# Order of the output accumulators in memory, and the activations of the first three groups, in a one-core decoder block

## The chip, the core and the metric

The kernel runs on one core of a Trainium2 chip. Its engines are TensorE (PE, matrix products into the accumulator memory PSUM; PEld is its weight load), VectorE (DVE), ScalarE (ACT), GpSimd (POOL) and SyncE (SP, which only issues transfers). Each has its own instruction queue and takes it strictly in order; they wait for each other by semaphores. The metric is the device time of one execution in microseconds, lower being better.

## The reference

One decoder block on 512 tokens of width 2048, all in float32. A pooling mixer and a stick-breaking attention are merged and added to `x`; what matters here is the squared-ReLU MLP at the end, with `w_ff1` of 2048 x 8192 and `w_ff2` of 8192 x 2048:

```
h2 = rms_norm(x, norm2_w[l]) * (1.0 + scale2[:, None]) + shift2[:, None]
f = jnp.square(jax.nn.relu(h2 @ w_ff1[l])) @ w_ff2[l]
x = x + gate2[:, None] * f
```

## The kernel before

**Precision and products.** A float32 operand is split into a high and a low part (`split_into`, lines 138 and 139: ScalarE writes `hi`, VectorE writes `lo = src - hi`), and a product is the sum of three, hi·hi, lo·hi and hi·lo. Both MLP products are done on 2 x 2 blocks with seven block products in place of eight (numbers `i` = 1, 7, 3, 6, 2, 5, 4; `PERIOD` sets that order), on sums of weight blocks (made by VectorE at line 1376 and by GpSimd's accumulating transfers at line 1354) and sums of activation blocks (`S`).

**Units.** The work is a list of units; a unit is one block product. For each unit `n` the main loop at the end of the kernel writes, in this order: what follows the unit before (`units[n-1].after()`), the split of the weights for unit `n+2` (`prep`; the ring of split weights has three places), one step of every open generator in the list `later` (`steps()`), and the matmuls of unit `n`. So an instruction that waits on ScalarE or VectorE holds up the weight splits behind it, and with three places in the ring TensorE runs dry about two units later.

**First product.** It makes 32 groups of 256 hidden columns. Groups 0 to 2 (`FIRST` = 3) are made together by all eight products into banks named `C`, while the sums `S` are still being formed (`first_units`). `after()` at its end puts the ReLU of these three groups into tiles `hr` and appends one `finish` generator each to `later`. `finish` has three steps: squares on ScalarE (line 1150), three VectorE sums (lines 1152 to 1155), then the store of `hr` to the DRAM buffer `hd` (line 1157; from ScalarE's queue, and for the last group from GpSimd's). From group 3 on the seven products follow, each of eight pairs of matmuls (lines 1176 and 1178). `M` is a product's bank. Product 6 adds to the bank of product 1, and product 5 to that of 6, so each needs ScalarE's copy of the partial result first (line 1183: `p`, `z`, `u` after products 1, 7 and 6).

**Second product.** It runs over eight chunks `c` of 1024 hidden rows and two column pairs `n`; a product is two units of 12 matmuls each (lines 303 to 305). Its operands `S` are read back from `hd`. The results are summed in eight accumulators `acc2[m, b]`, each 4 KiB per partition, where `m` is the column pair and `b` one of `"11", "21", "12", "22"`. The first chunk is written by a ScalarE copy (line 1317), and later products are added by VectorE (line 1319). `open_sums` makes the accumulators in memory that the first product's pool `evac` gives back: two `hr` buffers of 8 KiB, five small copies (`p`, `z`, `u`), and the tile `c` of 8 KiB. A new tile waits only for those old tiles whose bytes it covers. In the pool, accumulators lie in the order in which they are made; first written in the run are (0, 11), (0, 22), (0, 21), (1, 11), (1, 22), (0, 12), (1, 21), (1, 12). The last group's `hr` is in the first of the two `hr` buffers, at the pool's lowest bytes.

Of the kernel before, what the change touches and what calls it, by code (L numbers as in the profile page):

```python
# [10 lines left out]
F32 = mybir.dt.float32  # L11
# [5 lines left out]
P = 128  # L17
T = 512
# [78 lines left out]
def block_kernel(ctx: ExitStack, tc: tile.TileContext, x, c, w_ada, b_ada, norm1_w, w_in, q_norm_w,  # L97
                 k_norm_w, w_pool, pool_scale, w_a_up, w_b_up, w_o, norm2_w, w_ff1, w_ff2, out):
    nc = tc.nc
# [15 lines left out]
    def name_of(name):  # L115
        count[0] += 1
        return f"{name}_{count[0]}"
# [864 lines left out]
    NP, GROUPS, CH, CP = 8, 32, 8, 4  # L982
    FIRST = 3
# [15 lines left out]
    hd = dram.tile([GROUPS, P, 7, 256], F32, name="hd")  # L999
# [28 lines left out]
    later = []  # L1028

    def steps():  # L1030
        for s in list(later):
            if next(s, s) is s:
                later.remove(s)
# [34 lines left out]
    def first_units():  # L1068
        banks = {}

        def before(m):
            def go():
                s = m // 2
                if m % 2 == 0:
                    if s < 3:
                        scale_bias(s + 1)
                    if s:
                        split_x(s - 1, ((7, 0), (6, 1), (5, 3)))
                else:
                    if s < 3:  # L1080
                        split_x(s + 1, AS_IS)
                    sums_x(s)
                    if s == 2:
                        split_x(0, ((3, 2),))
                        split_x(1, ((3, 2),))
            return go

        def part(wh, wl, at, g, m):

            for row in range(2):  # L1090
                if m == 0:
                    banks[g, row] = bank.tile([P, 2, 256], F32, tag="bank", name=name_of("C"))
                for k in range(2):
                    i = ((1, 2), (3, 4))[row][k]
                    hi, lo = (S[i, m // CP][:, a, m % CP, :] for a in range(2))
                    for q in range(2):
                        cols = slice((at + 2 * k + q) * P, (at + 2 * k + q + 1) * P)
                        products(banks[g, row][:, q, :], wh[:, cols], wl[:, cols], hi, lo, m == k == q == 0,
                                 m == NP - 1 and k == 1, skip_group_check=True)

        def mm(m):
            def go(wh, wl):
                for g in range(2):
                    part(wh, wl, 4 * g, g, m)
            return go

        def mm2(m):
            def go(wh, wl):
                for e in range(2):
                    part(wh, wl, 4 * e, 2, m + e)  # L1110
            return go

        def after():
            def relu(g, hr):
                nc.scalar.activation(hr[:, 1:3, :], banks[g, 0], AF.Relu)
                nc.scalar.activation(hr[:, 0:4:3, :], banks[g, 1], AF.Relu)
                later.append(finish(g, hr))
            relu(0, h_tile(0))
            split_x(3, ((7, 0), (6, 1), (5, 3)))
            split_x(2, ((3, 2),))  # L1120
            split_x(3, ((3, 2),))
            xts.close()
            pools["evac"] = pool(ffr, "evac", 1, "right")
            relu(1, h_tile(1))
            relu(2, h_tile(3))

        def src(gm):
            def load(raw, _):
                for i, (g, m) in enumerate(gm):
                    nc.sync.dma_start(raw[:, i * T:(i + 1) * T].rearrange("p (q n) -> p q n", n=P),  # L1130
                                      w_ff1[g, :, :, m, :].rearrange("q p n -> p q n"))
            return load

        made_of = []
        for m in range(NP):
            made_of.append(Unit(0, (0, m), src(((0, m), (1, m))), mm(m), None, before(m)))
            if m % 2:
                made_of.append(Unit(0, (0, m, 2), src(((2, m - 1), (2, m))), mm2(m - 1),
                                    after if m == NP - 1 else None))
        return made_of  # L1140
# [3 lines left out]
    def h_tile(g):  # L1144

        return (pools["evac"] if g % 2 else hrp).tile([P, 8, 256], F32, tag="hr", bufs=1 + g % 2, name=name_of("hr"))

    def finish(g, hr):

        nc.scalar.activation(hr[:, 0:4, :], hr[:, 0:4, :], AF.Square)  # L1150
        yield
        nc.vector.tensor_tensor(hr[:, 4:6, :], hr[:, 1:4:2, :], hr[:, 0:1, :].broadcast_to([P, 2, 256]),
                                op=ALU.subtract)
        nc.vector.scalar_tensor_tensor(hr[:, 6, :], hr[:, 5, :], -1.0, hr[:, 1, :], op0=ALU.mult, op1=ALU.subtract)
        nc.vector.scalar_tensor_tensor(hr[:, 7, :], hr[:, 2, :], -1.0, hr[:, 6, :], op0=ALU.mult, op1=ALU.subtract)
        yield
        (nc.gpsimd if g == GROUPS - 1 else nc.scalar).dma_start(hd[g], hr[:, 1:8, :])


    def ff1_units(first):  # L1160
# [70 lines left out]
    keep, acc2 = {}, {}  # L1231
# [34 lines left out]
    def ff2_units(gn, i):  # L1266
        c, n = divmod(gn, 2)
        st = ff2_state.setdefault(gn, {})
        name = {1: "11", 2: "11", 6: "21", 4: "21", 5: "22", 7: "22", 3: "12"}[i]
        new = i in (1, 7, 2)  # L1270
        last = gn == 2 * CH - 1 and i == 3

        def open_sums():
            while later:
                steps()
            ffr.close()
            accp = pool(ffr, "acc2", 1, "right")
            for m in range(2):
                for b in ("11", "21", "12", "22"):
                    acc2[m, b] = accp.tile([P, 2, T], F32, name=f"acc_{m}{b}")  # L1280

        def mm_of(half):
            def mm(wh, wl):
                if "bank2" not in pools:
                    ffb.close()
                    pools["bank2"] = pool(ffb, "bank2", 4, space=PSUM)
                if half == 0:
                    if gn == 0 and len(made) < 7:
                        next_first()
                    if new:  # L1290
                        st[CHAIN[i]] = pools["bank2"].tile([P, 2, T], F32, tag="bank", name=name_of("M"))
                    if last:
                        a = acc2[n, name]
                        nc.vector.tensor_tensor(a, a, gated(2 * n + 1), op=ALU.mult)
                        nc.vector.tensor_tensor(a, keep[0, 2 * n + 1], a, op=ALU.subtract)  # L1295
                if half and n == 1 and c + 1 < CH:
                    make_s(i, c + 1)
                for t in range(2):
                    for k in range(2):
                        hi, lo = (S[i, c][:, a, 2 * half + k, t * P:(t + 1) * P] for a in range(2))  # L1300
                        cols = slice(k * T, (k + 1) * T)
                        products(st[CHAIN[i]][:, t, :], hi, lo, wh[:, cols], wl[:, cols], new and half == k == 0,
                                 half == k == 1, skip_group_check=not new)
            return mm

        def after():
            if not acc2:
                open_sums()
            ps, a = st[CHAIN[i]], acc2[n, name]
            if last:  # L1310
                for t in range(2):
                    nc.vector.tensor_tensor(ps[:, t, :], ps[:, t, :], keep["g", 2 * n + 1], op=ALU.mult)  # L1312
                    nc.vector.tensor_tensor(a[:, t, :], a[:, t, :], ps[:, t, :], op=ALU.subtract)  # L1313
                    nc.sync.dma_start(out[t * P:(t + 1) * P, T * (2 * n + 1):T * (2 * n + 2)], a[:, t, :])
                return
            if c == 0 and i in (1, 6, 7, 3):
                nc.scalar.activation(a, ps, AF.Copy)
            else:
                nc.vector.tensor_tensor(a, ps, a, op=ALU.add)  # L1319
            if c == CH - 1 and i in (2, 4, 5, 3):  # L1320
                put(0 if i in (2, 3) else 1, 2 * n + (i in (5, 3)), a)
            if gn == 0:
                load_s(i, 1)
            if n == 1 and c + 2 < CH:
                load_s(i, c + 2)
            elif n == 1 and c + 2 == CH and i in (1, 7, 6, 2, 5):
                hold((1, 7, 6, 2, 5).index(i), i)

        def src_of(half):
            return lambda raw, q: w_ff2[c, n, q, :, 2 * half:2 * half + 2, :].rearrange("p m n -> p (m n)")  # L1330
        return [Unit(i, (2, gn, half), src_of(half), mm_of(half), after if half else None) for half in range(2)]
# [122 lines left out]
```

## Time and profile before

| what | value |
|---|---|
| median of 3 runs | 2504.03 us (2501.37 to 2513.46) |
| the profiled execution, whole | 2503.11 us |
| its span, first to last instruction | 2501.4 us |
| mean granted TensorE clock | 0.994 |
| PE, DVE, ACT, POOL busy | 98%, 73%, 45%, 6% of the span |

The profile is of one execution. TensorE is busy in almost all of the span, so what counts is the few stretches in which it stands still or is granted less than its full clock. In the views below a row's bracket tells how long that engine stood idle just before the row, and what ended the idle time.

### The profile page before, as it was taken

Reading aid. Unit: us, or ns where it says so; the run is one execution under the profiler, and the core shown is the slowest. Engines: PE = TensorE matmul, PEld = TensorE weight load, DVE = VectorE, ACT = ScalarE, POOL = GpSimd, SP = SyncE. Lnnn points to the kernel's source line nnn. Section 1 sums busy time; section 2 is a strip of 40 time slices with the busy share of each in tenths; the row PEclk is TensorE's granted clock in tenths of the full one; section 3 lists DMA queues with packets and bytes.
Section 4 is the critical chain, followed back from the end, with each engine's and each line's share of the span. In section 5 each row is a group of like instructions: output and inputs, shape, how many; then the busy total and the mean of one; then the engine's idle time right before and its main releaser. Section 6 shows DMA issues by size and latency. Waiting matters only on the chain. (4 is left out here: it accounts for less than half of the span.)

```text
span 2501.4 us, 32636 instructions
## 1 busy us (share of the span) xinstructions
PE 2458.4 (98%) x12387; PEld 2055.6 (82%) x12387; DVE 1837.5 (73%) x2303; ACT 1134.1 (45%) x1552; POOL 155.7 (6%) x234
## 2 busy tenths in 40 slices
PE   8999999999999999999999999999998999999998
PEld 5777888888888888888888888888886888888886
DVE  5888555555667666665577777777786889888889
ACT  5222556653223222433455555555555444444452
POOL 0000011100000000000000100001010100100100
PEclk9999999999999999999999999999998999999999
DMA  9873222223667667576447777777787777877775
GB/s 314 267 244 98 88 68 69 75 79 108 227 221 233 227 226 239 192 235 228 127 130 200 208 210 216 211 210 203 212 256 230 212 227 211 219 201 207 214 224 150
DMA packets 246037, 482.48 MB, mean 193 GB/s; under 512 B 16684, under 2 KB 111972, under 8 KB 245880
## 3 DMA queue, kind: packets, MB, share of 16 engines
q1 hardware_dynamic: 222232, 382.80, 46.6%
q0 software_dynamic: 19184, 69.15, 14.8%
q10 hardware_dynamic: 4464, 28.44, 2.8%
q8 instruction: 97, 1.59, 0.3%
q14 instruction: 60, 0.49, 0.1%
HBM read 442.59 MB, written 37.75 MB: 192 GB/s over the span
## 5 line engine op out<-in xcount | busy, mean ns | idle before, releaser
L139 DVE TENSOR_TENSOR flo<-raw,fhi 128x1024 fp32r<-128x1024 f32 x439 | 534.4, 1221 | 213.9 <-ACT fhi L138 213.7
L138 ACT ACTIVATE fhi<-raw 128x1024 fp32r<-128x1024 f32 x439 | 464.4, 1058 | 395.5 <-PE M L305 295.7
L1176 PE MATMUL M<-S,fhi 128*128 128x512 f32 x1624 | 566.3, 395 | 3.7 <-ACT u L1183 3.1
L138 ACT ACTIVATE whi<-raw 128x512 fp32r<-128x512 f32 x388 | 236.9, 627 | 487.3 <-PE ps L304 148.5
L1178 PE MATMUL M<-S,flo 128*128 128x256 f32 x1624 | 451.2, 278 | 0.0
L139 DVE TENSOR_TENSOR wlo<-raw,whi 128x512 fp32r<-128x512 f32 x388 | 263.4, 690 | 214.1 <-ACT whi L138 213.1
L1176 PEld LDWEIGHTS M<-S,fhi 128*128 128x128 f32 x1624 | 305.9, 188 | 75.5 <-ACT u L1183 3.5
L303 PE MATMUL M<-fhi,S 128*128 128x512 f32 x896 | 349.8, 390 | 11.0 <-ACT fhi L138 11.0
L303 PE MATMUL ps<-hh,whi 128*128 128x512 f32 x896 | 354.9, 396 | 2.2 <-ACT whi L138 2.2
L304 PE MATMUL M<-flo,S 128*128 128x512 f32 x896 | 350.3, 391 | 1.6 <-DVE flo L139 1.6
L305 PE MATMUL ps<-hh,wlo 128*128 128x512 f32 x896 | 350.0, 391 | 0.0
L304 PE MATMUL ps<-hl,whi 128*128 128x512 f32 x896 | 349.6, 390 | 0.0
L305 PE MATMUL M<-fhi,S 128*128 128x512 f32 x896 | 349.5, 390 | 0.0
L1178 PEld LDWEIGHTS M<-S,flo 128*128 128x128 f32 x1624 | 306.4, 189 | 0.0
L408 DVE SCALAR_TENSOR_TENSOR ada<-raw,sc,ada 128x512 f32<-128x512 f32 (+1 forms) x296 | 207.2, 700 | 41.7 <-DMA raw<-in_w_ada_dram 34.8
L303 PEld LDWEIGHTS M<-fhi,S 128*128 128x128 f32 x896 | 168.9, 188 | 46.5 <-ACT fhi L138 11.4
L303 PEld LDWEIGHTS ps<-hh,whi 128*128 128x128 f32 x896 | 168.4, 188 | 42.7 <-issue 6.5
L304 PEld LDWEIGHTS M<-flo,S 128*128 128x128 f32 x896 | 168.7, 188 | 39.0 <-DVE flo L139 4.4
L305 PEld LDWEIGHTS ps<-hh,wlo 128*128 128x128 f32 x896 | 168.4, 188 | 36.5 <-DVE wlo L139 0.3
L305 PEld LDWEIGHTS M<-fhi,S 128*128 128x128 f32 x896 | 168.8, 188 | 35.1
L304 PEld LDWEIGHTS ps<-hl,whi 128*128 128x128 f32 x896 | 168.6, 188 | 33.4
L1354 POOL DMA_DIRECT2D raw<-in_w_ff_dram x122 | 107.4, 953 | 1136.8 <-DVE raw L1376 439.1
(260 smaller groups left out, 3214.5 us busy)
## 6 DMA issues: line engine op xcount, KB each, us to landing
raw<-in_w_ff_dram SPq DMA_DIRECT2D x244, 512.0 KB, 5.2
raw<-in_w_ada_dram SPq DMA_DIRECT2D x128, 512.0 KB, 4.4
raw<-in_w_ff_dram POOLq DMA_DIRECT2D x122, 512.0 KB, 7.7
raw<-in_w_in_dram SPq DMA_DIRECT2D x94, 512.0 KB, 4.1
raw<-in_w_ada_dram SPq DMA_DIRECT2D x128, 256.0 KB, 5.9
S<-hd SPq DMA_DIRECT2D x56, 512.0 KB, 6.9
hd<-hr ACTq DMA_DIRECT2D x31, 896.0 KB, 3.6
raw<-in_w_in_dram SPq DMA_DIRECT2D x64, 256.0 KB, 3.1
```

The costliest lines, as they stand in the source:

```text
L138: nc.scalar.activation(hi, src, AF.Copy)
L139: nc.vector.tensor_tensor(lo, src, f(hi), op=ALU.subtract)
L303: nc.tensor.matmul(ps, lhsT=lh, rhs=rh, start=start, stop=False, **kw)
L304: nc.tensor.matmul(ps, lhsT=lh, rhs=rl, start=False, stop=False, **kw)
L305: nc.tensor.matmul(ps, lhsT=ll, rhs=rh, start=False, stop=stop, **kw)
L408: nc.vector.scalar_tensor_tensor(s, raw, sc[:, k:k + 1], before, op0=ALU.mult, op1=ALU.add)
L1176: nc.tensor.matmul(ps, lhsT=wh[:, cols], rhs=both, start=new and m == 0, stop=False, skip_group_check=not new)
L1178: nc.tensor.matmul(ps[:, 256:T], lhsT=wl[:, cols], rhs=both[:, 0, :], start=False, stop=m == NP - 1, skip_group_check=not new)
L1354: nc.gpsimd.dma_start(raw[u.key, what], u.src(None, q), accum_op=ALU.add)
```

## The change

Three edits. `open_sums` makes the eight accumulators in another order, so that each lies at another place of the same 32 KiB. `finish` takes a number of empty steps to pass before the squares, 0, 2 and 4 for groups 0, 1 and 2. And the stores of groups 0 to 2 are issued by GpSimd.

```
-            relu(0, h_tile(0))
+            relu(0, h_tile(0), 0)
...
-            relu(1, h_tile(1))
-            relu(2, h_tile(3))
+            relu(1, h_tile(1), 2)
+            relu(2, h_tile(3), 4)
...
-    def finish(g, hr):
-
+    def finish(g, hr, wait=0):
+
+        for _ in range(wait):
+            yield
...
-        (nc.gpsimd if g == GROUPS - 1 else nc.scalar).dma_start(hd[g], hr[:, 1:8, :])
+        (nc.gpsimd if g < FIRST or g == GROUPS - 1 else nc.scalar).dma_start(hd[g], hr[:, 1:8, :])
...
-            for m in range(2):
-                for b in ("11", "21", "12", "22"):
-                    acc2[m, b] = accp.tile([P, 2, T], F32, name=f"acc_{m}{b}")
+            for m, b in ((1, "12"), (1, "21"), (1, "22"), (0, "12"), (1, "11"), (0, "21"), (0, "22"), (0, "11")):
+                acc2[m, b] = accp.tile([P, 2, T], F32, name=f"acc_{m}{b}")
```

The program has the same instructions; TensorE's and SyncE's orders stay as they were. ScalarE where groups 0 to 2 end and group 3 begins, before (`hr_11267`, `hr_11284` and `hr_11287` are groups 0, 1 and 2; `fhi` are weight splits):

```order
L138 ACTIVATE fhi_11290<-raw_10788 128x1024
L1150 ACTIVATE hr_11267<-hr_11267 128x1024
L1150 ACTIVATE hr_11284<-hr_11284 128x1024
L1150 ACTIVATE hr_11287<-hr_11287 128x1024
L1183 ACTIVATE p_2173_11314<-M_11297 128x512
L138 ACTIVATE fhi_11316<-raw_10854 128x1024
L1183 ACTIVATE z_2178_11350<-M_11333 128x512
L138 ACTIVATE fhi_11352<-raw_10720 128x1024
L1157 DMA hd<-hr_11267 128x1792
L1157 DMA hd<-hr_11284 128x1792
L1157 DMA hd<-hr_11287 128x1792
L1183 ACTIVATE u_2182_11377<-M_11297 128x512
```

and now, where lines from 1150 on carry a number two higher:

```order
L138 ACTIVATE fhi_11290<-raw_10788 128x1024
L1152 ACTIVATE hr_11267<-hr_11267 128x1024
L1185 ACTIVATE p_2173_11312<-M_11295 128x512
L138 ACTIVATE fhi_11314<-raw_10854 128x1024
L1185 ACTIVATE z_2178_11342<-M_11325 128x512
L138 ACTIVATE fhi_11344<-raw_10720 128x1024
L1152 ACTIVATE hr_11284<-hr_11284 128x1024
L1185 ACTIVATE u_2182_11368<-M_11295 128x512
L138 ACTIVATE fhi_11370<-raw_10788 128x1024
L138 ACTIVATE fhi_11398<-raw_10908 128x1024
L1152 ACTIVATE hr_11287<-hr_11287 128x1024
```

Two of the three squares moved behind the copies `p` and `z` and the splits between them, and the three stores left this queue. GpSimd at the same place, before (sums of weight blocks by transfer):

```order
L1354 DMA raw_10788<-in_w_ff_dram 128x1024
L1354 DMA raw_10720<-in_w_ff_dram 128x1024
L1354 DMA raw_10977<-in_w_ff_dram 128x1024
L1354 DMA raw_10908<-in_w_ff_dram 128x1024
L1354 DMA raw_11356<-in_w_ff_dram 128x1024
```

and now:

```order
L1355 DMA raw_10977<-in_w_ff_dram 128x1024
L1159 DMA hd<-hr_11267 128x1792
L1159 DMA hd<-hr_11284 128x1792
L1355 DMA raw_10908<-in_w_ff_dram 128x1024
L1159 DMA hd<-hr_11287 128x1792
L1355 DMA raw_11348<-in_w_ff_dram 128x1024
```

The stores stand in front of the weight sums of the next groups. On VectorE each group's three sums moved with its square: the two splits that stood behind all nine sums now stand behind the first three. ScalarE where the second product begins, before, with the semaphores that each instruction waits for (`hr_2932` is the last group; `acc_011` is the accumulator (0, 11)):

```order
L1190 ACTIVATE hr_2932_16394<-hr_2932_16394 128x512 [waits DVE_49]
L1191 ACTIVATE hr_2932_16394<-hr_2932_16394 128x512
L1150 ACTIVATE hr_2932_16394<-hr_2932_16394 128x1024 [waits Activation_49]
L1317 ACTIVATE acc_011_16444<-M_2933_16402 128x1024 [waits DVE_49,DMASW4_49,PE_49,Activation_49]
L138 ACTIVATE fhi_2937_16455<-raw_2896_16177 128x1024
L1220 ACTIVATE S2_2919_16306<-S2_2919_16306 128x1024 [waits DMAHW2_49]
L138 ACTIVATE fhi_2940_16474<-raw_2907_16230 128x1024 [waits PE_49]
L1317 ACTIVATE acc_022_16447<-M_2939_16461 128x1024 [waits PE_49]
```

and now:

```order
L1192 ACTIVATE hr_2932_16394<-hr_2932_16394 128x512 [waits DVE_49]
L1193 ACTIVATE hr_2932_16394<-hr_2932_16394 128x512
L1152 ACTIVATE hr_2932_16394<-hr_2932_16394 128x1024 [waits Activation_49]
L1318 ACTIVATE acc_011_16451<-M_2933_16402 128x1024 [waits PE_49]
L138 ACTIVATE fhi_2937_16455<-raw_2896_16177 128x1024
L1222 ACTIVATE S2_2919_16306<-S2_2919_16306 128x1024 [waits DMAHW7_49]
L138 ACTIVATE fhi_2940_16474<-raw_2907_16230 128x1024 [waits DVE_49,PE_49]
L1318 ACTIVATE acc_022_16450<-M_2939_16461 128x1024 [waits PE_49]
```

The order is the same; the copy into (0, 11) no longer names the semaphore of GpSimd's transfer (DMASW), on which the last group's store reports. In the new order (1, 12) and (1, 21) lie where that group's `hr` was.

## Rows read from the trace of the kernel before

**Rows 1.** The page: span, TensorE's busy time (us, share, instructions), one group of part 5.

```profile
span 2501.4 us, 32636 instructions
...
PE 2458.4 (98%) x12387; PEld 2055.6 (82%) x12387; DVE 1837.5 (73%) x2303; ACT 1134.1 (45%) x1552; POOL 155.7 (6%) x234
...
L139 DVE TENSOR_TENSOR flo<-raw,fhi 128x1024 fp32r<-128x1024 f32 x439 | 534.4, 1221 | 213.9 <-ACT fhi L138 213.7
```

**Rows 2.** Waits of TensorE: engine, line <- releaser: us in total, times, longest.

```profile
PE M L303 <- ACT fhi L138: 11.0, 1, 11.0
...
PE M L1176 <- ACT u L1183: 3.1, 1, 3.1
...
PE M L304 <- DVE flo L139: 1.6, 5, 0.5
...
PE M L1176 <- ACT p L1183: 0.6, 1, 0.6
```

**Rows 3.** Timeline of ScalarE, 1286 to 1335 us: start, us, engine, line, operation [idle before].

```profile
1296.00 2.97 ACT L1150 ACTIVATE hr<-hr 128x1024 f32<-128x1024 f32 x3
...
1298.85 0.61 ACT L1183 ACTIVATE p<-M 128x512 f32<-128x512 f32 x1
...
1307.81 0.60 ACT L1183 ACTIVATE u<-M 128x512 f32<-128x512 f32 x1 [5.97 <-DVE hr L1155]
...
1325.96 1.05 ACT L138 ACTIVATE fhi<-raw 128x1024 fp32r<-128x1024 f32 x1
```

**Rows 4.** Timeline of VectorE, 1286 to 1312 us.

```profile
1302.72 0.68 DVE L1152 TENSOR_TENSOR hr<-hr 128x512 f32<-128x512 f32 x1
```

**Rows 5.** Timeline of TensorE, 1286 to 1318 us.

```profile
1299.96 0.40 PE L1176 MATMUL M<-S,fhi 128*128 128x512 f32 x1
...
1304.82 0.40 PE L1176 MATMUL M<-S,fhi 128*128 128x512 f32 x1
...
1308.46 0.80 PE L1176 MATMUL M<-S,fhi 128*128 128x512 f32 x1 [3.13 <-ACT u L1183]
...
1314.87 0.40 PE L1176 MATMUL M<-S,fhi 128*128 128x512 f32 x1
```

**Rows 6.** Busy time by window; the last three columns: granted clock, DMA share, GB/s.

```profile
1310.00:1315.00 5.00, 5.00 (x18) 4.29 (x18) 3.18 (x5) 1.36 (x2) 0.00 (x0) 0.53 1.01 340
...
1875.00:1885.00 10.00, 0.00 (x0) 0.00 (x0) 0.00 (x0) 1.53 (x2) 0.25 (x1) 0.64 0.92 281
...
1885.00:1890.00 5.00, 4.04 (x9) 2.86 (x10) 4.27 (x4) 5.00 (x6) 0.00 (x0) 0.50 0.00 0
...
1905.00:1915.00 10.00, 10.00 (x46) 8.29 (x45) 7.53 (x7) 4.65 (x5) 0.03 (x1) 1.00 1.05 322
```

**Rows 7.** Timeline of all engines, 1862 to 1895 us.

```profile
1871.41 0.39 PE L305 MATMUL M<-fhi,S 128*128 128x512 f32 x1
...
1873.70 0.42 DVE L1155 SCALAR_TENSOR_TENSOR hr<-hr 128x256 f32<-128x256 f32 x1
...
1874.13 0.39 PE L305 MATMUL M<-fhi,S 128*128 128x512 f32 x1
...
1874.69 0.56 POOL L1157 DMA_DIRECT2D hd<-hr  x1 [0.69 <-issue]
...
1883.47 1.03 ACT L1317 ACTIVATE acc<-M 128x1024 f32<-128x1024 f32 x1 [12.11 <-DMA hd<-hr]
...
1885.49 0.79 PE L303 MATMUL M<-fhi,S 128*128 128x512 f32 x1 [10.97 <-ACT fhi L138]
...
1891.57 0.40 PE L303 MATMUL M<-fhi,S 128*128 128x512 f32 x1
```

**Rows 8.** The stores of line 1157, 31 from ScalarE's queue and one from GpSimd's.

```profile
DMA to landing us min/median/max: 3.5/3.6/8.7
```

**Rows 9.** GpSimd's transfers of line 1354: its timeline, and landing from 1292 to 1340 us.

```profile
1317.88 1.76 POOL L1354 DMA_DIRECT2D raw<-in_w_ff_dram  x2 [24.51 <-DVE raw L1376]
...
DMA to landing us min/median/max: 5.3/6.9/9.4
```

More of the change, by code (lines that the diff above doesn't have):

```diff
@@ L1113, in after, with relu @@
         def after():
-            def relu(g, hr):
+            def relu(g, hr, wait):
                 nc.scalar.activation(hr[:, 1:3, :], banks[g, 0], AF.Relu)
                 nc.scalar.activation(hr[:, 0:4:3, :], banks[g, 1], AF.Relu)
-                later.append(finish(g, hr))
-            relu(0, h_tile(0))
+                later.append(finish(g, hr, wait))
+            relu(0, h_tile(0), 0)
             split_x(3, ((7, 0), (6, 1), (5, 3)))
```

## Prediction

> **What bounds the kernel now.** I read the page first: TensorE is busy 98% of the span [rows 1], so the kernel is as long as TensorE's work plus the stretches in which it stands still or runs at a lower clock. The waits of TensorE come next, since they tell which stretches these are. Two of them touch the change: 11.0 us in one wait, ended by a weight split on ScalarE, and 3.1 us plus 0.6 us, ended by the copies `u` and `p` of line 1183 [rows 2]. The reader is to see that each of the two long ones is a single wait, and that the matmuls of the MLP have besides them only five waits for the low split, of at most 0.5 us. The timelines then tell what stands behind each.
>
> *At the beginning of the first product* ScalarE squares three groups in one piece (2.97 us), and `p` comes behind them at 1298.85 [rows 3]. Later `u` stands idle 5.97 us, for VectorE's last sum of `hr` [rows 3]: it isn't `u` itself that waits, but the three stores ahead of it in ScalarE's queue, and they wait for nine sums that VectorE begins at 1302.72 [rows 4]. TensorE needs `u` for product 5 and starts it at 1308.46, after 3.13 us of idleness [rows 5]. It restarts at half clock: the granted clock is 0.53 from 1310 to 1315 [rows 6].
>
> *At the beginning of the second product* the copy into accumulator (0, 11) waits 12.11 us on ScalarE for the store of the last group's `hr` [rows 7], which lies on the same bytes. The store was issued at 1874.69 and needs 8.7 us [rows 7, 8]. Behind the copy stands the weight split of the fifth unit, so TensorE stops after the matmul of 1874.13 and goes on at 1885.49 [rows 7], at a granted clock of 0.50, the lower level [rows 6], until the matmul of 1891.57 is at full speed again.
>
> **The change part by part.** Sums are made against the profiled execution: 2503.1 us, of which 2501.4 is the span [rows 1]. The median of the three runs is 2504.0, 0.9 above it.
>
> *Squares in turn, and stores moved to GpSimd.* Full speed is 0.347 us for a pair of matmuls: 14 pairs from 1299.96 to 1304.82 [rows 5]. The pair after 1304.82 was due at 1305.17. Ten pairs, 3.47 us of work, would have ended at 1308.64; the eleventh starts at 1314.87 [rows 5]. The loss is 6.2 us, 3.1 of it idleness and 3.1 of it half clock. With 0.6 for `p` the place costs 6.8 us.
>
> Now only one square (2.97 / 3 = 1.0 us) stands ahead of `p`, which comes some 2 us sooner, so the 0.6 goes. `u` has no store ahead of it and waits for TensorE alone. What comes late next? On VectorE the split for product 5 used to come behind nine sums and now comes behind three; a group's three take about 1.5 us, from 1302.72 to 1307.4 for nine, so the split ends near 1303.6, ahead of the 1304.4 at which TensorE comes to product 5 when the 0.6 of `p` is gone too. The squares of groups 1 and 2, 1.0 us each, lie in front of `u` and of a split; ScalarE has waited 5.97 us there until now, so they are covered. If that cover were gone, each would cost its 1.0 us. I cost the squares at nothing, and take the whole 6.8. The bounds are 0 and 6.8.
>
> *The three stores on GpSimd.* They are three of the 31 that ScalarE issued. On GpSimd's queue they wait for the sums of their group, and behind the second waits the weight sum that was issued at 1317.88, which itself waited for VectorE [rows 9]. The second group's sums are through by about 1306, and the weight sum's own input on VectorE, two splits and three small sums later by the order, comes some 5 us after that by my estimate, so the queue is free by then. The buffers are wanted again from group 3 on, a whole round of seven products of 2.8 us later, and a store needs 3.5 to 8.7 us [rows 8]. I cost them at nothing; the upper bound is one more stall like today's, 6.2 us.
>
> On whether GpSimd is a good place: the only store from its queue took 8.7 us, against a median of 3.6 over all 31 plus that one [rows 8], but with DMA at 0.92 of its time [rows 6], so the row doesn't tell queue from load. The Trainium skill (SBUF — State Buffer, section "SBUF: two separate sides") speaks against this edit: descriptors of transfers issued from GpSimd are written by GpSimd itself, a VectorE operation in a two-port mode locks it out, and it advises the ScalarE or SP queue. By that rule the stores and the weight sum behind them would be late, which is the third rival below; by the row alone they are not.
>
> *The accumulators.* At full speed 12 matmuls, one unit, take 2.72 us (1871.41 to 1874.13 [rows 7]). The next unit was due at 1874.36 and would have ended at 1877.08; the unit after it starts at 1891.57. The loss is 14.5 us: 11.1 of standing and 3.4 of half clock. Now (0, 11) lies on the upper half of tile `c`, whose last reader has finished before the squares of the last group, which stand ahead of the copy on ScalarE in any case. The copy then runs when its product is done.
>
> What is late next there is VectorE. Its last sum of `hr` starts at 1873.70 and ends at 1874.12 [rows 7], and the low split for the stopped unit comes behind it, 1.22 us [rows 1]: 1875.34. The unit's second matmul wants it at 1874.58, so 0.76 us stays. That is no longer than waits which TensorE has today without a lower clock (0.5 and 0.6 [rows 2]). Net gain 13.7.
>
> The accumulators that now lie on the last group's `hr` are (1, 21) and (1, 12). The copy into (1, 21) follows some twenty units after the start, near 1874.4 + 16 x 2.72 = 1918; the store lands near 1883.4. Nothing waits.
>
> What cover is lost? During the standstill DMA moved 281 GB/s over 10 us, 2.8 MB, and from 1885 to 1890 it rested [rows 6]. Now the next units run beside those transfers. From 1905 to 1915 the DMA share is 1.05 [rows 6], so there isn't much room, yet TensorE there waits for nothing. I take 0.5 us of short waits; the bounds are 0 and one stall with its half clock, 6.2.
>
> Sum: 6.8 + 13.7 - 0.5 = 20.0. 2503.1 - 20.0 = 2483.1, some 2484 if the 0.9 of the median counts. I say 2483.
>
> **The rivals.**
> 1. *Only a part of the second gain stays.* Weight sums for the next column pair come late, because their loads run beside the backlog. For it: the full DMA share of 1.05 [rows 6], landing times of 5.3 to 9.4 us for such sums [rows 9]. Against: no wait of TensorE or of a split there is put down to a transfer today. One stall with lowered clock gives 6.2 back: 2489.
> 2. *The change doesn't do what it says at the accumulators*: another old tile on the new bytes is still in use, and the copy waits as before. Only 6.8 is won: 2496. Against: the copy's waits now name TensorE alone.
> 3. *GpSimd's queue is late in the first product.* The weight sum behind the stores feeds the split that ScalarE makes at 1325.96 today, 8.1 us after the sum's issue at 1317.88, with 6.9 us as the median landing [rows 3, 9]. That is a margin of 1.2. With the stall gone the split moves ahead by 6.8, VectorE's input by some 5 (my estimate, from the order and the durations above), and any further delay on GpSimd beyond that margin lets TensorE wait: 3.1 plus 3.1 again, 2489.
> 4. *Slower than before: DMA sets the pace in the first two column pairs.* If the 2.8 MB cannot be moved beside the rest, the 14.5 us come back as waits, but in pieces; each piece long enough to lower the clock costs another 3.1. Eight pieces: 2503.1 - 6.8 + 8 x 3.1 = 2521. It decides from three pieces on (9.3 against 6.8). Against: the rest of 5 us after the standstill shows that the transfers had room to spare.
>
> **How the numbers follow.** My forecast gets 0.74 (its own range 2478 to 2487), rival 1 gets 0.10, rival 2 0.06, rival 3 0.06, rival 4 0.04. Half a per cent, about what a measurement of this kernel can tell from no change, is 12.5 us, so faster means below 2491.5. The forecast lies there, and most of rivals 1 and 3, whose spread reaches the bound: 0.74 + 0.08 + 0.04 = 0.86 for faster, 0.10 for the same (rival 2 and the remainders), 0.04 for slower. The range is 2477 to 2493: at the low end both losses go without rest and the runs fall a little under the profiled one, and the top takes in rivals 1 and 3 with a small margin. Rivals 2 and 4 stay out.
>
> **What would show it.** Right: TensorE's wait for `u` and its wait of 11.0 us are gone, and the granted clock is 1.00 in the windows of rows 6 shifted by 7 to 20 us; a wait of some 0.8 us for the low split (line 139) stands at the beginning of the second product; ScalarE's copy into (0, 11) starts right behind the last square. Wrong: ScalarE's copies still wait for a store; TensorE has new waits for splits whose weights had not landed, first 25 to 45 us behind the beginning of the second product; or a new wait near product 5 of group 4, with GpSimd's weight sums late.

## The result, and the profile after

| what | before | after |
|---|---|---|
| median, us | 2503.31 (10 runs, 2500.80 to 2513.84) | 2494.74 (10 runs, 2492.45 to 2495.75) |
| profiled execution, whole | 2503.11 | 2492.45 |
| its span | 2501.4 | 2490.7 |
| mean granted TensorE clock | 0.994 | 0.998 |

The ratio is 0.9946, with a 95% interval of 0.9931 to 0.9962. The kernel is faster by 8.6 us in the medians (0.34%) and by 10.7 between the two profiled executions; the ratio, which goes by all runs, says 0.54%. 20.0 us had been predicted, and the median lies 1.7 above the range of 2477 to 2493. The three numbers differ because the kernel before has times of two groups: of its 49 timed runs, beside after and the experiments, 33 lie between 2500.4 and 2505.4 and 16 between 2511.5 and 2517.5. The profiled execution belongs to the lower group; what parts the two is found below.

The page of after, for [rows 1]: the busy time of TensorE has grown by 4.2 us, though it has the same instructions.

```profile
span 2490.7 us, 32638 instructions
...
PE 2462.6 (99%) x12387; PEld 2056.5 (83%) x12387; DVE 1836.8 (74%) x2303; ACT 1134.3 (46%) x1552; POOL 157.0 (6%) x237
```

The waits of TensorE from 1290 us to the end, after, for [rows 2]. The 11.0, the 3.1 and the 0.6 are gone; nothing has come in their place.

```profile
PE M L304 <- DVE flo L139: 1.1, 4, 0.5
```

ScalarE's timeline of after at the beginning of the first product (start, us), for [rows 3]. One square stands ahead of `p`, and `u` waits 0.33 us for TensorE, where it waited 5.97 for VectorE.

```profile
1296.64 1.08 ACT L1152 ACTIVATE hr<-hr 128x1024 f32<-128x1024 f32 x1
1297.59 0.62 ACT L1185 ACTIVATE p<-M 128x512 f32<-128x512 f32 x1
...
1302.45 0.60 ACT L1185 ACTIVATE u<-M 128x512 f32<-128x512 f32 x1 [0.33 <-PE M L1180]
```

The timeline of all engines of after where the second product begins, for [rows 7]. The copy into (0, 11) comes right behind the last square, with no wait for the store, which is issued only at 1878.76.

```profile
1874.37 1.06 ACT L1152 ACTIVATE hr<-hr 128x1024 f32<-128x1024 f32 x1
1875.34 1.01 ACT L1318 ACTIVATE acc<-M 128x1024 f32<-128x1024 f32 x1
...
1878.12 1.22 DVE L139 TENSOR_TENSOR flo<-raw,fhi 128x1024 fp32r<-128x1024 f32 x1
...
1878.52 0.39 PE L303 MATMUL M<-fhi,S 128*128 128x512 f32 x1
...
1878.76 0.56 POOL L1159 DMA_DIRECT2D hd<-hr  x1 [0.68 <-ACT S L1222]
...
1879.39 0.50 PE L304 MATMUL M<-flo,S 128*128 128x512 f32 x1 [0.49 <-DVE flo L139]
```

What is left of the standstill is the 0.49 us for the low split. Windows of after, for [rows 6] (last three columns: granted clock, DMA share, GB/s). The clock is full in all four. DMA is full in the last three, and TensorE stands still in none of them beyond those 0.49 us.

```profile
1310.00:1315.00 5.00, 5.00 (x31) 4.34 (x30) 4.74 (x7) 2.30 (x3) 2.26 (x3) 1.00 0.80 252
1875.00:1885.00 10.00, 9.51 (x43) 7.54 (x42) 9.90 (x12) 8.11 (x10) 1.44 (x2) 1.00 1.08 291
1885.00:1890.00 5.00, 5.00 (x24) 4.14 (x23) 5.00 (x6) 3.81 (x4) 0.00 (x0) 1.00 0.99 356
1905.00:1915.00 10.00, 10.00 (x46) 8.29 (x45) 7.95 (x8) 7.99 (x9) 1.73 (x2) 1.00 1.03 253
```

So both stalls went, and with them all that they cost. Where did ten microseconds stay? The view of one line's instructions tells it (count, ns min/median/max, first and last start). Before, the high matmuls of the first product and one line of the second:

```profile
L1176 PE MATMUL M<-S,fhi x1624: 392/395/796, 1293.1 to 1863.1; 128*128 128x512 f32 x181
...
L305 PE MATMUL M<-fhi,S x896: 387/389/628, 1863.9 to 2493.4; 128*128 128x512 f32 x180
```

and after:

```profile
L1178 PE MATMUL M<-S,fhi x1624: 395/398/403, 1293.8 to 1867.2; 128*128 128x512 f32 x181
...
L305 PE MATMUL M<-fhi,S x896: 387/389/397, 1868.1 to 2483.0; 128*128 128x512 f32 x180
```

The second product went from 629.5 to 614.9 us, 14.6 less. The first went from 570.0 to 573.4: 3.4 *more*, though 6.8 of waiting and half clock left it. So its matmuls as such take about 10 us longer. Groups by shape, TensorE, in the 460 us from 1320 to 1780, far from both edits (count | busy us, mean ns | idle before); before:

```profile
L1176 PE MATMUL M<-S,fhi 128*128 128x512 f32 x1328 | 460.4, 394 | 0.0
```

and after:

```profile
L1178 PE MATMUL M<-S,fhi 128*128 128x512 f32 x1303 | 460.4, 399 | 0.0
```

Without a wait in either, 1328 pairs of matmuls start in that time before and 1303 after: 460.4 / 1328 = 0.3467 us for a pair, and 460.4 / 1303 = 0.3533. The stage has 1624 pairs, so the difference is 1624 x 0.00667 = 10.8 us, or 10.4 for the 195 units (of eight pairs) that stand at the fast pace in the profile before. That is what is missing. A unit takes 2.77 us at the one pace and 2.83 at the other; below these are called fast and slow.

### The profile page after: what moved, and what is told of

Same layout as the page of the kernel before. It is cut to its first block, busy times and chain, and to the rows that moved or that the text cites. A ratio compares the mean times of both kernels' runs of the same rounds, so it can differ in the third digit from the quotient of the medians.

```text
span 2490.7 us, 32638 instructions
## 1 busy us (share of the span) xinstructions
PE 2462.6 (99%) x12387; PEld 2056.5 (83%) x12387; DVE 1836.8 (74%) x2303; ACT 1134.3 (46%) x1552; POOL 157.0 (6%) x237
## 4 chain that ended last, share of the span: by engine, by line
PE 95%; DVE 2%; DMA 1%; issue 1%; ACT 0%; SPq 0%; POOL 0%; DVEq 0%; ACTq 0%
PE M L1178 15%; PE ps L303 15%; PE ps L305 14%; PE ps L304 14%; PE M L1180 8%; PE M L304 7%; PE M L305 7%; PE M L303 7%; PE st L397 1%; PE C L304 1%; PE C L305 1%; PE C L303 1%; DVE flo L139 1%; PE pm L429 1%; DMA x<-in_x_dram 0%
## 5 line engine op out<-in xcount | busy, mean ns | idle before, releaser
L1178 PE MATMUL M<-S,fhi 128*128 128x512 f32 x1624 | 573.9, 399 | 0.0
```

What stands on the lines that cost most here:

```text
L1178: nc.tensor.matmul(ps, lhsT=wh[:, cols], rhs=both, start=new and m == 0, stop=False, skip_group_check=not new)
```

## The experiments

A *hold* is a wait of TensorE in this stage. In the edits, `...` and words in brackets stand for code that is left out. The theories, by the letters that the texts on record use: A says that the missing time is this pace, and that it hangs on the holds; A2 is its form in which the held matmul decides (after a hold at the high matmul of a pair fast, at the low one slow); A4 is its last form: either pace may follow a hold, whatever the kernel, and without a hold the stage keeps the slow pace in which it begins. The rivals: A3 says that the pace is set once, where the stage begins, or only by a hold with lowered clock; B that the stores on GpSimd and the squares in turn cost the time as such; C that the new place of the accumulators costs it.

**The new order of the accumulators alone** (before with this one edit).

```diff
-            for m in range(2):
-                for b in ("11", "21", "12", "22"):
-                    acc2[m, b] = ...
+            for m, b in ((1, "12"), (1, "21"), (1, "22"), (0, "12"), (1, "11"), (0, "21"), (0, "22"), (0, "11")):
+                acc2[m, b] = ...
```

> Only the accumulators' order is changed. Theory A (two paces of TensorE in the first product: a pair of matmuls takes 0.3533 us as the stage begins and 0.3467 after a wait has interrupted the stream; the changed kernel has no wait there and keeps the slow pace over 1624 pairs, 10.8 us): both waits at the beginning of the first product stay, pace 0.3467, and only the second product's 14 us go: about 2489.5, 14 below before and some 5 below the changed kernel. Theory B (the 10 us are lost to the stores on GpSimd and the squares in turn as such, for instance by contention): also 2489.5, pace 0.3467. Theory C (the accumulators' place slows something): pace or second product slower than that, 2493 or more.

Measured: 2489.61 (2488.67 to 2490.09), before beside it 2503.14, ratio 0.9940 (0.9919 to 0.9962). The waits for `u` (3.0) and `p` (0.6) are still there, and behind them the pace is fast:

```profile
L1176 PE MATMUL M<-S,fhi 128*128 128x512 f32 x1328 | 460.4, 394 | 0.0
```

One edit alone is 5.1 us faster than all three together, and theory C falls. 2503.14 - 2489.61 = 13.5; the prediction had 13.7 less 0.5 for this part. Four runs at the fast pace can be chance, though: the first product is that of the kernel before, of whose 49 runs 16 lie some 10 us higher. By these shares an estimate for many runs is 2489.6 + 16/49 x 10.4 = 2493.0, little below all three edits.

**The squares in turn and the stores on GpSimd alone** (after with the old order of the accumulators).

```diff
-            for m, b in ((1, "12"), ...):
+            for m in range(2):
+                for b in ("11", "21", "12", "22"):
```

> Only the squares in turn and the stores on GpSimd; the accumulators lie as before. Theories A and B: the waits of 0.6 and 3.1 us and the half clock go (6.8 us), the pace stays at 0.3533 and costs 10.3: about 2507, some 3.5 slower than before. Theory C: pace 0.3467, 2496.

Measured: 2507.55 (2504.84 to 2509.40), ratio 1.0007 (0.9991 to 1.0023). Waits of TensorE:

```profile
PE M L303 <- ACT fhi L138: 10.8, 1, 10.8
```

The long wait is back as expected, the two short ones are gone, and all 202 units are slow. This part, for which 6.8 us had been predicted, gains nothing: 10.4 for the pace less 6.8 makes 3.6 us slower, and 2507.55 lies 4.4 above 2503.14. Against the upper group of the kernel before (2512.79 to 2517.54 beside it) it is at least 5.2 faster.

**Squares at once, their sums in turn** (after, with the squares ahead of the empty steps), so that `p` is late again but `u` is not.

```diff
-        for _ in range(wait):
-            yield
         nc.scalar.activation(hr[:, 0:4, :], hr[:, 0:4, :], AF.Square)
         yield
+        for _ in range(wait):
+            yield
```

> The changed kernel, but the three squares are made in one piece ahead of the copy p, as before; the VectorE sums stay in turn and the stores on GpSimd. Theory A: p comes late, TensorE waits about 0.6 us for it, the pace after that is 0.3467; 0.6 + 0 instead of 10.3 lost: about 2483 to 2484, 10 below the changed kernel. Theory B: the stores are still on GpSimd, the pace stays at 0.3533: 2493 to 2494.

Measured: 2494.40 (2484.64 to 2496.14), ratio 0.9957 (0.9942 to 0.9972). A miss, but an instructive one. Seven runs lie at 2493.58 or above, and one at 2484.64, where the expectation was. In the profiled one (2493.58) the hold for `p` is there and one fast unit follows it; then the timeline of TensorE reads:

```profile
1305.95 0.39 PE L1178 MATMUL M<-S,fhi 128*128 128x512 f32 x1
1306.29 0.39 PE L1180 MATMUL M<-S,flo 128*128 128x256 f32 x1
1306.51 0.39 PE L1178 MATMUL M<-S,fhi 128*128 128x512 f32 x1
```

The low matmul starts 0.34 us behind the high one, where 0.23 to 0.24 is the rule: a hold of 0.11, too short for the list of waits. The next high one starts 0.22 behind it, 0.10 late again. From there on all units are slow. So a hold can take the fast pace away as well.

**All eight high matmuls of a unit, then all eight low ones** (after).

```diff
-                for m in range(NP):
-                    (high matmul m, low matmul m)
+                for low in range(2):
+                    for m in range(NP):
+                        (low matmul m if low else high matmul m)
```

> The changed kernel, but in the first product's units of groups 3 to 31 the eight matmuls with the high weights come first and then the eight with the low ones, in place of pairs; same matmuls, same sums in another order. Theory A, if the slow pace belongs to the alternation of long and short matmuls: 16 matmuls take 8 x 0.3467 = 2.77 us without any wait, about 2482. Theory A, if the slow pace belongs to any stream that begins without a wait: 8 x 0.3533 = 2.83 us, 2494. Theory B: 2.83 us as well, 2494.

Measured: 2487.45 (2486.32 to 2488.25), ratio 0.9933 (0.9907 to 0.9959), between the two expectations. All 202 units of the profiled execution take 2.79 us, with no hold, and the four runs lie within 2 us: this order showed one pace, 0.02 above the fast one.

**A long hold at a high matmul in the middle** (after; copy `u` of group 17 made seven times).

```diff
-                nc.scalar.activation(st[name], st[CHAIN[i]], AF.Copy)
+                for _ in range(7 if name == "u2" and g == 17 else 1):
+                    nc.scalar.activation(st[name], st[CHAIN[i]], AF.Copy)
```

> The changed kernel, with the copy u of group 17 made seven times over, so that TensorE is held for some 1 us at the first (high, 512 columns wide) matmul of a pair, in the middle of the first product, with its weights long split. Theory A2 (a hold at the high matmul of a pair leaves the fast pace behind it): units of 2.83 us before that place and of 2.77 behind it to the end, some 105 units, 5.5 us won less the hold: about 2489 to 2490. Theory A3 (the pace is set once, where the stage begins, or only by a hold with lowered clock): 2.83 throughout, 2494 to 2495.

Measured: 2492.24, one run. The hold, two weight loads 11 us behind it, and later a tiny hold of 0.10 at a low matmul, in the timeline of TensorE:

```profile
1585.18 0.50 PE L1178 MATMUL M<-S,fhi 128*128 128x512 f32 x1 [1.64 <-ACT u L1186]
...
1596.48 0.19 PEld L1178 LDWEIGHTS M<-S,fhi 128*128 128x128 f32 x1
1596.70 0.19 PEld L1180 LDWEIGHTS M<-S,flo 128*128 128x128 f32 x1
...
1790.80 0.39 PE L1178 MATMUL M<-S,fhi 128*128 128x512 f32 x1
1791.13 0.39 PE L1180 MATMUL M<-S,flo 128*128 128x256 f32 x1
```

Groups by shape for 1320 to 1570, 1600 to 1780 and 1800 to 1860:

```profile
L1178 PE MATMUL M<-S,fhi 128*128 128x512 f32 x709 | 250.6, 399 | 0.0
...
L1178 PE MATMUL M<-S,fhi 128*128 128x512 f32 x520 | 180.3, 391 | 0.0
...
L1178 PE MATMUL M<-S,fhi 128*128 128x512 f32 x171 | 60.5, 399 | 0.0
```

That is 0.3535, 0.3467 and 0.3538 us a pair: slow, fast, slow again behind the tiny hold. The long hold itself left the slow pace: its own unit and the three behind it, to 1596.6, are slow. The pace turns in the next unit, at a granted clock of 1.00, and is fast for 68 units from 1599.4 on. That unit's first low weights are loaded 0.22 us behind the high ones, where 0.12 is the rule, and VectorE's low splits stand just ahead of them (two in 2.35 us from 1595.44). So a hold of 0.1 us is the likely trigger, and probably itself an effect of the seven copies; that is argued, not shown. A2 wanted the fast pace at once and to the end, A3 the slow one throughout: both missed. 68 x 8 x 0.00667 = 3.6 gained less 1.64 of waiting is 2.0 below after's 2494.74, and 2.5 was measured. In this one run a wait of 1.64 us more makes the kernel no slower.

**A long hold at a low matmul in the middle** (the first experiment's kernel; the low split for product 6 of group 17 made five times).

```diff
-    def split_w(raw):
+    def split_w(raw, again=0):
...
         split_into(raw, hi, lo)
+        for _ in range(again):
+            nc.vector.tensor_tensor(lo, raw, f(hi), op=ALU.subtract)
...
-            ready[n] = split_w(raw[u.key, what])
+            ready[n] = split_w(raw[u.key, what], 4 if u.key[:2] == (1, 14) and u.i == 6 else 0)
```

> The kernel with only the accumulators' order changed (fast pace behind its waits), with the low split of product 6 of group 17 made five times over by VectorE, so that TensorE is held at the second (low, 256 columns wide) matmul of a pair. Theory A2 (a hold at the low matmul leaves the slow pace): units of 2.77 us before that place and 2.83 behind it, 5.5 us lost and the hold on top: 2495 to 2496. Theory A3: 2.77 throughout, 2490 to 2491.

Measured: 2498.01, one run. The hold in the timeline:

```profile
1581.81 0.39 PE L1180 MATMUL M<-S,flo 128*128 128x256 f32 x1 [2.16 <-DVE flo L1010]
```

and groups by shape for 1320 to 1570 and 1600 to 1850:

```profile
L1178 PE MATMUL M<-S,fhi 128*128 128x512 f32 x722 | 250.3, 391 | 0.0
...
L1178 PE MATMUL M<-S,fhi 128*128 128x512 f32 x709 | 250.6, 399 | 0.0
```

Fast until the hold, slow for the 101 units behind it: 2489.61 + 2.16 + 101 x 8 x 0.00667 = 2497.2. The granted clock is 1.00 from 1581 to 1585, so a hold in the middle, with the clock full, changed the pace, and A3 is out.

**Sums one step later** (the kernel with squares at once; empty steps 1, 3 and 5 in place of 0, 2 and 4), to keep the tiny hold away from the hold for `p`.

```diff
-            relu(0, h_tile(0), 0)
+            relu(0, h_tile(0), 1)
...
-            relu(1, h_tile(1), 2)
-            relu(2, h_tile(3), 4)
+            relu(1, h_tile(1), 3)
+            relu(2, h_tile(3), 5)
```

> The squares in one piece as in the run with squares at once, but the VectorE sums of groups 0, 1 and 2 pass one more step, so that the low split of product 5 comes ahead of them and TensorE isn't held at it. Theory A2: the hold of 0.6 at p sets the fast pace and nothing unsets it: units of 2.77 us, 2483 to 2484, 10 below the changed kernel. Theory A3: as in the run with squares at once, 2494.

Measured: 2495.85 (2484.57 to 2497.52), ratio 0.9934 (0.9912 to 0.9957). Three of nine runs lie between 2484.6 and 2485.2, six between 2494.5 and 2497.5. The profiled one is of the upper group: the hold for `p` stands there, and slow units follow it at once. So a hold at a high matmul does not always leave the fast pace, and A2 falls, as the long hold in the middle had shown already.

```profile
L1178 PE MATMUL M<-S,fhi 128*128 128x512 f32 x1303 | 460.4, 399 | 0.0
```

**The same kernel again**, for a profile of the other outcome.

> The kernel with squares at once and later sums, looked at once more. Theory A4: near 2485 with units of 2.77 us behind the hold at p, or near 2496 with 2.83, as in its first profile.

Measured: 2485.76, one run, and fast behind the same hold for `p` of 0.6 us:

```profile
L1178 PE MATMUL M<-S,fhi 128*128 128x512 f32 x1328 | 460.4, 391 | 0.0
```

One program, one hold, both paces: A4 is what is left. B falls too, since the stores are on GpSimd here and the stage is fast. Farther on this execution has a tiny hold of the kind behind which two others turned slow, if a smaller one (the low matmul 0.27 us behind the high one, the next high one 0.22 behind that), and it stays fast:

```profile
1785.47 0.39 PE L1178 MATMUL M<-S,fhi 128*128 128x512 f32 x1
1785.74 0.39 PE L1180 MATMUL M<-S,flo 128*128 128x256 f32 x1
1785.96 0.40 PE L1178 MATMUL M<-S,fhi 128*128 128x512 f32 x1
```

**The kernel before again**, twice, for a profile of its upper group.

> The kernel before, unchanged, looked at once more. Theory A4 (which of the two paces follows a wait is not fixed by the kernel, but by the instant at which the stream is let go): the time is near 2503 with units of 2.77 us in the first product, or near 2513 with units of 2.83; no other pairing. If near 2513 comes with units of 2.77, the 10 us lie elsewhere.

> The same as the run before it: 2503 with units of 2.77 us, or 2513 with units of 2.83.

Measured: 2511.86 and 2512.11, one run each, both in the upper group; both have the holds for `p` (0.6) and `u` (3.1 and 3.0), and 197 slow units behind them. Groups by shape for the first of them, 1320 to 1780:

```profile
L1176 PE MATMUL M<-S,fhi 128*128 128x512 f32 x1303 | 460.4, 399 | 0.0
```

So the two groups of the kernel before are the two paces, as far as one profile of the lower and two of the upper show it. The view of single lines for the same execution:

```profile
L1176 PE MATMUL M<-S,fhi x1624: 390/398/795, 1294.0 to 1872.9; 128*128 128x512 f32 x181
...
L305 PE MATMUL M<-fhi,S x896: 387/389/628, 1873.7 to 2502.1; 128*128 128x512 f32 x180
```

At the same pace, then, the change is worth 2511.86 - 2492.45 = 19.4 us between the profiled executions. That of after is its fastest run; from the median of the 16 upper runs (2513.3) to after's median it is 18.6.

**High, high, low, low** (after, with the matmuls of a unit two by two), since another order had shown one pace.

```diff
-                for m in range(NP):
+                for low, m in [(low, m + j) for m in range(0, NP, 2) for low in range(2) for j in range(2)]:
...
-                    (high matmul m, low matmul m)
+                    (low matmul m if low else high matmul m)
```

> The changed kernel with the order of matmuls high, high, low, low in place of high, low. No theory of mine gives the pace of this order: at the fast pace's 2.773 us a unit without any hold it would be 2482, at the pace of eight high and eight low (2.793) 2486, at the slow one 2494. It tells whether an order of the matmuls alone holds the fast pace.

Measured: 2485.61 (2484.85 to 2486.92), before beside it 2508.76, ratio 0.9907 (0.9872 to 0.9942). Groups by shape, 1320 to 1780:

```profile
L1182 PE MATMUL M<-S,fhi 128*128 128x512 f32 x1321 | 414.9, 395 | 0.0
```

All 202 units take 2.79 us, and the four runs lie in one group. By its median this is the fastest kernel of the study; its runs and those of after (2492.45 to 2495.75) don't overlap, though they were not made side by side.

**High, high, low, low with the accumulators' order alone**, to size the squares in turn and the stores on GpSimd where the pace did not change (the first experiment's kernel with the matmuls two by two).

> The accumulators' new order and high, high, low, low, but the first groups' squares and stores as before. If the order of matmuls fixes the pace, this shows what the first edit is worth by itself: the waits of 0.6 and 3.1 us and the half clock come back, 6.8 us over the run with high, high, low, low and both edits: 2492 to 2493. If the pace still depends on a wait, it comes out at another time by some 4 us.

Measured: 2492.88 (2491.10 to 2493.29), ratio 0.9953 (0.9937 to 0.9969). The waits for `p` (0.6) and `u` (3.1) are there, and the units take 2.79 before and behind them:

```profile
L1180 PE MATMUL M<-S,fhi 128*128 128x512 f32 x1321 | 414.9, 395 | 0.0
```

2492.88 - 2485.61 = 7.3 us is what the squares and stores are worth at one pace, measured in two sessions; 6.8 had been predicted.

## Where the prediction was right, and where it failed

**The step that failed** is the first term of the sum, 6.8: "Full speed is 0.347 us for a pair of matmuls", read from the 14 pairs behind the hold for `p`, "and take the whole 6.8". The step took that pace for the matmuls' own and let it stand when the holds go. It was the pace *behind a hold*. The trace of before shows the other one ahead of it, in the timeline of TensorE that the prediction had read from 1299.96 on only:

```profile
1293.13 0.40 PE L1176 MATMUL M<-S,fhi 128*128 128x512 f32 x1
...
1298.43 0.40 PE L1176 MATMUL M<-S,fhi 128*128 128x512 f32 x1
```

15 pairs in 5.30 us, 0.353 each, and 0.347 from the hold on. After has no hold, and it kept what it began with: 570.0 - 6.8 + 10.4 = 573.6, and 573.4 was measured. So the term came out at -3.4 in place of +6.8. Its bounds, "0 and 6.8", had no room for it either; a stage of 1624 equal pairs makes 10.8 us of 6.7 ns each.

**Squares and stores otherwise.** Right: `p` and `u` come in time, the 6.8 is there (7.3 at one pace), the squares of groups 1 and 2 cost nothing.

**The accumulators.** Right: 13.7 less 0.5 predicted, 14.6 in the second product's length, 13.5 with this edit alone. The remaining wait for the low split is 0.49 where 0.76 was worked out. (0.76 is not "no longer" than waits of 0.5 and 0.6, as the prediction has it; that the clock stays full is shown only for the 0.49.)

**DMA.** Right, and a little too careful: the shares of 1.08, 0.99 and 1.03 go with no wait of TensorE beyond 0.5 us, so the 0.5 is not seen.

**The rivals.** The missing time is none of them. Rival 2 (copy waits as before) is out by the timeline at 1875.34; rivals 1 and 4 by the list of waits. Rival 3 (GpSimd's queue late): the weight sum behind the stores was issued earlier than before, not later [rows 9]. GpSimd's timeline of after:

```profile
1312.14 0.89 POOL L1355 DMA_DIRECT2D raw<-in_w_ff_dram  x1 [4.18 <-ACT fhi L138]
```

and the three stores landed within (us, minimum, median, maximum)

```profile
DMA to landing us min/median/max: 4.9/6.0/7.3
```

where the same three, from ScalarE's queue, before took

```profile
DMA to landing us min/median/max: 4.8/5.7/6.6
```

The median of 3.6 over all stores [rows 8] is no measure for this place; side by side the queue makes at most 0.7 us. The Trainium skill (SBUF — State Buffer, section "SBUF: two separate sides") warns that VectorE, in an operation of a two-port mode, keeps GpSimd from writing the descriptors of its transfers, and advises the ScalarE or SP queue. These three stores show next to nothing of it, though no row tells whether VectorE ran such an operation then. The view of the three names nobody that waits for them.

**The range and the chances.** Faster by over half a per cent, with 0.86, is only just borne out by the ratio (0.54%), and its interval holds the bound; the median of 2494.74 lies above the 2491.5 that the prediction drew for it. By the ratio the time would be 0.9946 x 2503.31 = 2489.8, inside the range, but that is luck: the ratio gains by the three of ten runs before that lie in the upper group, and the sum had been made against an execution of the lower one. A rival "the first product stays at the pace that it begins with" was missing. Worked out from the two paces in the trace of before, it would have given 2483 + 10.4 = 2493.4, and the range would have reached further up. A sign of two groups stood in the table before, too: one of its three runs took 2513.46.

## What to carry to other kernels

The price of a wait is not its length alone: before a wait is priced, compare the pace of the same instructions ahead of it and behind it, and multiply any difference by the rest of the stage. Here two waits, 3.7 us together, were removed, and the faster rhythm that had followed them over most of 1624 pairs went too. A wait put in for the rhythm's sake is no remedy, for the same wait left either pace. Another order of the same instructions (here two by two) showed one pace in all its runs, and by the medians it was worth more. And where a kernel's times fall in two groups, profile one of each before a change is sized against either.

## What the hardware showed that was not expected

- Pairs of a 512-column and a 256-column matmul run at 0.3467 or 0.3533 us, steadily for hundreds of units, at a granted clock of 1.00 and with weight loads of 188 ns at the median in both. In the starts of the trace the slow pace repeats every three pairs, 1.06 us; three pairs of the fast one take 1.04. Without a hold it stayed slow (all ten runs of after lie in 3.3 us). Where it changed there was a hold, once of 0.1 us only; but not every hold changed it. What in the engine keeps a pace, and what decides which one follows a hold, is open: no row shows it, and no experiment took it apart.
- In the orders high, high, low, low and all high then all low the same sixteen matmuls take 2.79 us, between 2.77 and 2.83, and the runs lie in one group (four, four and seven runs of three kernels).
- The half clock behind the same wait for `u` lasts differently: the window from 1310 to 1315 has a granted clock of 0.53 in the profiled execution before [rows 6] and 0.77 in the one repeated:

```profile
1310.00:1315.00 5.00, 5.00 (x25) 4.34 (x24) 3.91 (x5) 2.23 (x3) 0.00 (x0) 0.77 0.98 334
```
